# Second expert product in groups of eight blocks, two-bank sums, 32 lead tiles, and a moved broadcast of expert numbers

## The chip, the cores and the metric

The kernel runs on one core of one Trainium2 chip. The metric is the device time of one execution in microseconds; the time before is 3585.99 us, the median of three runs (3580.31, 3585.99 and 3586.01).

## The reference, cut to what matters

The model is one decoder block on 512 tokens of width 2048: a token mixer (convolution branch and state-space branch), then an expert mixer, then a final norm. The change touches the expert mixer alone. Each token picks 128 of 16384 single-neuron experts:

```python
best, pos = lax.top_k(cand, PEER_TOPK)            # 8 heads x 16 experts a token
expert = jnp.take_along_axis(cand_idx, pos, axis=-1)
gates = jax.nn.softmax(best, axis=-1)
act = jax.nn.gelu(jnp.einsum('td,thkd->thk', xb, u_tab[expert]))
out = jnp.einsum('thk,thkd->td', gates * act, v_tab[expert])
```

All is float32; the tables u and v have 16384 rows of 2048 numbers each (128 MB a table).

## The kernel before, in words

The token mixer and the routing (`route_half`, `top16`) take the first part of the span. The expert mixer then treats the 512 tokens in two ways at once.

**Dense tokens.** For the last 352 tokens (`ND`) every expert is computed, in 128 tiles of 128 experts (`NE`). `dense_u(j)` (line 858) multiplies tile j of table u with the tokens: 16 steps of 3 matmuls of 128x352 (lines 235 to 237), since each float32 product is made of a high and a low part (`split`, line 203: ACT casts the high part, DVE or POOL subtracts it to give the low part). ACT's Gelu gives `ga`. `weigh(j)` (line 1075) multiplies `ga` with the gates of the tile and splits the product into `wh` and `wl`. `dense_v(g, dc, ws)` (line 1117) multiplies four such tiles (`GRP` = 4) with a quarter `dc` of the width of table v: 48 matmuls of 128x352 into four one-bank sums (`ps_v`, 6 buffers), which DVE then adds to `acc` in SBUF one bank at a time (line 59, four additions of 128x352).

Until the gates exist, nothing can be weighed, so the first `LEAD` = 24 tiles run as `dense_u` alone and store `ga` in DRAM (`d_ga`). After `LAG` = 6 of them `transp_routes` turns the expert numbers and gates, and `gate_steps` then builds the dense gate matrix (4 tokens a step, 88 steps: one-hot products of 128x128 on PE, line 907) in the matmul stream of the next 16 tiles, and writes it to `d_g`. When the lead is over, groups 0 to 4 of `dense_v` run back to back (their tiles are re-read by `reload`), and from group 5 on one `dense_u` and one `dense_v` alternate.

**Gathered tokens.** For the first 160 tokens the 128 chosen rows are gathered: `gather_block` (line 967) is a generator whose steps are advanced by `pump_rows` between the dense units. A step issues one indirect DMA of 128 rows (1 MB, POOL's queue, line 963) two steps ahead and lets DVE multiply the oldest row tile (line 1011 for u, line 1022 for v). Three row buffers (`NROW`) serve the gathers, the token rows and the norm's scratch. `turn` makes token rows from columns with 16 PE transposes (line 985) each time a pass begins. The rows of one indirect DMA are held back behind `pace[0]`, the last elementwise POOL instruction recorded.

**Queues.** Each engine runs its own queue in order, but the framework that builds the queues may put a ready instruction ahead of one that is recorded earlier and still waits; the recorded order is a priority. SP issues the loads of both tables (line 222), the reloads (line 920) and the loads of token columns (line 973). POOL issues the gathers, the gate loads `gq` (line 1073) and `spread`, which copies 32 tokens' expert numbers over four partition groups through DRAM (lines 823 and 825). In the kernel before `spread(eidb, d_eb, eid1)` is recorded right after `expert_ids(eid1, 1)`, that is, before the first `dense_u`. The low parts of the first `UPOOL` = 10 tiles are made on POOL, as are every second low part of table v and the product with the gates (line 1081).

Of the kernel before, what the change touches and what calls it, by code (L numbers as in the profile page):

```python
# [15 lines left out]
T = 512  # L16
# [4 lines left out]
TB = 4  # L21
# [13 lines left out]
LEAD = 24  # L35
# [3 lines left out]
LAG = 6  # L39
GM = 1  # L40
TAIL = 2
NR = 18
NROW = 3
RLEAD = 1.5
RV = 1.0
UPOOL = 10
GRP = 4
# [106 lines left out]
def kernel(ctx, tc, xT, vecs, cst, w_in, conv_w_out, w_vg, w_out, w_q, keysT,  # L154
# [7 lines left out]
    vec = const.tile([128, V_END], F32, name="vec")  # L162
    cs = const.tile([128, C_END], F32, name="cs")
    ones = const.tile([128, 128], F32, name="ones")
# [11 lines left out]
    d_g = dram.tile([ND // 32, NE // GRP, 128, GRP, 32], F32, name="d_g")  # L176
    d_eb = dram.tile([GB, 128], I32, name="d_eb")
    d_gb = dram.tile([GB, 128], F32, name="d_gb")
    d_ga = [dram.tile([128, ND], F32, name=f"d_ga{j}") for j in range(LEAD)]

    yst = ExitStack()
# [44 lines left out]

    def proj_steps(ps, srcs, ah, al, eng=None, side=0.0):
        nk = 8 * len(srcs)
        for k in range(nk):
            if k % 8 == 0:  # L230
                hi, lo = load_w(srcs[k // 8], eng[k // 8] if isinstance(eng, tuple) else eng)
# [47 lines left out]
    rstd1 = const.tile([128, T], F32, name="rstd1", tag="rstd")  # L279
# [74 lines left out]
    rho4 = const.tile([128, 32], F32, name="rho4")  # L354
    ew = const.tile([128, 2, 224], F32, name="ew")
# [318 lines left out]
    rstd2 = const.tile([128, T], F32, name="rstd2", tag="rstd")  # L674
# [35 lines left out]

    scst = ExitStack()
    scp = scst.enter_context(tc.tile_pool(name="scp", bufs=8, reuse_waits="tile"))
    ij = const.tile([128, 2, TB, 8, 16], F32, name="ij")
    gt = const.tile([128, TB, 8, 16], F32, name="gt")
# [85 lines left out]
    zs = const.tile([128, TB * 8], F32, name="zs")  # L800

    def softmax():
# [5 lines left out]
        _mul(nc, g, g, zs[:, :, None].to_broadcast([128, TB * 8, 16]))  # L808

    eidx = con2.tile([128, HK], I32, name="eidx")  # L810
    eidb = con2.tile([128, GB], I32, name="eidb")
    gtb = con2.tile([128, GB], F32, name="gtb")
    sel = con2.tile([128, GB], F32, name="sel")
# [7 lines left out]
    def spread(o, d, src):  # L821

        nc.gpsimd.dma_start(d, src[:GB])
        for c in range(REP):
            nc.gpsimd.dma_start(o[c * GB:(c + 1) * GB, :], d[:, c * 32:(c + 1) * 32])

    eid1 = con2.tile([128, HK], I32, name="eid1")
    expert_ids(eidx, 0)
    expert_ids(eid1, 1)
    spread(eidb, d_eb, eid1)  # L830
# [8 lines left out]
    rp = ctx.enter_context(tc.tile_pool(name="rp", bufs=NR, side="right", reuse_waits="tile"))  # L839
    rowp = ctx.enter_context(tc.tile_pool(name="rowp", bufs=1, side="right", reuse_waits="tile"))  # L840
# [3 lines left out]
    def ps_v(shape=(512,)):  # L844
        return pp.tile([128, *shape], F32, name="pv", tag="v", bufs=6)
# [12 lines left out]
    def dense_u(j, eng=None, mid=None):  # L858
        pu = pp.tile([128, ND], F32, name="pu", tag="u", bufs=2)
        proj(pu, full(peer_ut, j), h2h, h2l, eng, mid=mid)  # L860
# [6 lines left out]
    tT = [ring(f"tT{i}") for i in range(3)]  # L867

    def transp_routes():
        softmax()  # L870
        spread(gtb, d_gb, gt[:, 1].rearrange("p h k -> p (h k)"))
# [29 lines left out]
    def gate_tokens(t0):  # L901
# [9 lines left out]
        if u0 == 28:  # L911
            for q in range(2):
                nc.sync.dma_start(d_g[t0 // 32, 16 * q:16 * q + 16].rearrange("q i j t -> i q (j t)"),
                                  stg[q].rearrange("p (q j) t -> p q (j t)", j=GRP))

    gars = {}

# [33 lines left out]
    def row_norm(o, x, g_dram):  # L951
# [4 lines left out]
        nc.vector.scalar_tensor_tensor(o, x, r, scr[:n], op0=ALU.mult, op1=ALU.mult)  # L956

    act = con2.tile([128, HK], F32, name="act")

# [7 lines left out]
    def gather_block(t0, n, ids, gates, steps):  # L967
        xt = [None]

        def load():  # L970
            xt[0] = row("xt").rearrange("p (k t) -> p k t", k=KD)
            if n == 128:
                nc.sync.dma_start(xt[0], d_x2[:, :, t0:t0 + 128].rearrange("k p t -> p k t"))
                return
            part = row("xp")[:, :KD * n].rearrange("p (k t) -> p k t", k=KD)
            nc.sync.dma_start(part, d_x2[:, :, t0:t0 + n].rearrange("k p t -> p k t"))
            for c in range(128 // n):
                nc.gpsimd.tensor_copy(xt[0][:, :, c * n:(c + 1) * n], part)

        def turn(scale):  # L980
            x2 = rowp.tile([128, D], F32, name="rows0", tag="rows", bufs=1)
            for q in range(4):
                pt = ps_v()
                for k in range(4):
                    nc.tensor.transpose(pt[:, k * 128:(k + 1) * 128], xt[0][:, 4 * q + k], ident)  # L985
                nc.scalar.activation(x2[:, q * 512:(q + 1) * 512], pt, AF.Copy, scale=scale)
            return x2

        load()
        for _ in range(3):  # L990
            yield
        x = turn(1.0)
        row_norm(x, x, gffn)
        todo = [(tab, e) for tab in (peer_u, peer_v) for e in range(steps)]
        live = []

        def ahead():
            if todo:
                tab, e = todo.pop(0)
                live.append(gather_row(tab, ids, e))  # L1000

        ahead()
        ahead()
        yield
        for i in range(steps):
            if i == steps - 2:
                load()
            else:
                ahead()
            g = live.pop(0)  # L1010
# [235 lines left out]
```

## Time and profile before

| | us |
|---|---|
| Time, median of three runs | 3585.99 |
| Profiled execution, own time | 3586.99 |
| Its span, first to last instruction | 3584.8 |
| First `dense_u` matmul | 1326.7 |
| Last `dense_v` matmul (then the last transposes and the norm) | 3567.9 |

The span is 2.2 us shorter than the profiled execution's own time, which is 1.0 us above the median. All positions below are microseconds from the span's first instruction.

### The profile page before, as it was taken

Reading aid. Unit: us, or ns where it says so; the run is one execution under the profiler, and the core shown is the slowest. Engines: PE = TensorE matmul, PEld = TensorE weight load, DVE = VectorE, ACT = ScalarE, POOL = GpSimd, SP = SyncE. Lnnn points to the kernel's source line nnn. Section 1 sums busy time; section 2 is a strip of 40 time slices with the busy share of each in tenths; the row PEclk is TensorE's granted clock in tenths of the full one; section 3 lists DMA queues with packets and bytes.
Section 4 is the critical chain, followed back from the end, with each engine's and each line's share of the span. In section 5 each row is a group of like instructions: output and inputs, shape, how many; then the busy total and the mean of one; then the engine's idle time right before and its main releaser. Section 6 shows DMA issues by size and latency. Waiting matters only on the chain. (4 is left out here: it accounts for less than half of the span.)

```text
span 3584.8 us, 50132 instructions
## 1 busy us (share of the span) xinstructions
PE 3416.8 (95%) x19091; PEld 3169.5 (88%) x19091; DVE 2856.6 (80%) x4147; ACT 1281.7 (36%) x2025; POOL 1452.8 (41%) x924
## 2 busy tenths in 40 slices
PE   8999999999999994997889999999999999999998
PEld 6888888888888884986789999999999999999998
DVE  7685848996535997796866999978999898797984
ACT  4234344325223331873223333333333333433333
POOL 1200000110003543343654666656666666465642
PEclk9999999999999997998899999999999999999999
DMA  5533444434444332699877989898989889897882
GB/s 176 154 108 114 129 123 123 140 125 129 135 147 132 113 111 69 188 302 320 273 252 264 357 333 355 340 337 317 356 347 343 335 342 358 285 361 295 344 303 95
DMA packets 261905, 845.30 MB, mean 236 GB/s; under 512 B 42640, under 2 KB 105184, under 8 KB 219904
## 3 DMA queue, kind: packets, MB, share of 16 engines
q1 hardware_dynamic: 189248, 433.25, 35.9%
q0 software_dynamic: 64352, 396.12, 29.4%
q10 hardware_dynamic: 8064, 12.72, 1.0%
q8 instruction: 150, 2.46, 0.3%
q14 instruction: 91, 0.75, 0.1%
HBM read 790.91 MB, written 51.09 MB: 235 GB/s over the span
## 5 line engine op out<-in xcount | busy, mean ns | idle before, releaser
L204 ACT CAST whi<-wraw 128x1024 fp32r<-128x1024 f32 x736 | 771.9, 1051 | 1792.1 <-PE pu L236 610.5
L205 DVE TENSOR_TENSOR wlo<-wraw,whi 128x1024 fp32r<-128x1024 f32 x556 | 743.1, 1351 | 207.6 <-ACT whi L204 206.5
L237 PE MATMUL pu<-h2h,wlo 128*128 128x352 f32 x2048 | 664.9, 325 | 67.7 <-POOL wlo L205 50.6
L1130 PE MATMUL pv<-wh,whi 128*128 128x352 f32 x2048 | 671.1, 328 | 47.8 <-DVE acc L59 29.9
L1132 PE MATMUL pv<-wh,wlo 128*128 128x352 f32 x2048 | 667.5, 326 | 4.7 <-DVE wlo L205 4.7
L235 PE MATMUL pu<-h2l,whi 128*128 128x352 f32 x2048 | 670.1, 327 | 1.1 <-ACT whi L204 1.1
L1131 PE MATMUL pv<-wl,whi 128*128 128x352 f32 x2048 | 667.5, 326 | 0.0
L236 PE MATMUL pu<-h2h,whi 128*128 128x352 f32 x2048 | 660.2, 322 | 0.0
L205 POOL TENSOR_TENSOR wlo<-wraw,whi 128x1024 fp32r<-128x1024 f32 x180 | 446.9, 2484 | 178.0 <-ACT whi L204 169.8
L1011 DVE SCALAR_TENSOR_TENSOR grow<-grow,rows 128x2048 f32<-128x2048 f32 x160 | 421.2, 2635 | 95.0 <-DMA grow<-in_peer_u_dram,eidx 83.3
L1022 DVE SCALAR_TENSOR_TENSOR rows<-grow,act,rows 128x2048 f32<-128x2048 f32 x160 | 427.8, 2674 | 85.1 <-DMA grow<-in_peer_v_dram,eidx 61.7
L237 PEld LDWEIGHTS pu<-h2h,wlo 128*128 128x128 f32 x2048 | 387.9, 189 | 71.9 <-POOL wlo L205 51.1
L1130 PEld LDWEIGHTS pv<-wh,whi 128*128 128x128 f32 x2048 | 390.9, 191 | 52.0 <-DVE acc L59 33.4
L1132 PEld LDWEIGHTS pv<-wh,wlo 128*128 128x128 f32 x2048 | 390.7, 191 | 5.1 <-DVE wlo L205 5.1
L1131 PEld LDWEIGHTS pv<-wl,whi 128*128 128x128 f32 x2048 | 392.4, 192 | 0.0
L235 PEld LDWEIGHTS pu<-h2l,whi 128*128 128x128 f32 x2048 | 386.8, 189 | 2.4 <-ACT whi L204 1.6
L236 PEld LDWEIGHTS pu<-h2h,whi 128*128 128x128 f32 x2048 | 387.7, 189 | 0.0
L235 PE MATMUL ps<-hl,whi 128*128 128x512 f32 x896 | 353.3, 394 | 9.2 <-ACT whi L204 9.2
L237 PE MATMUL ps<-hh,wlo 128*128 128x512 f32 x896 | 350.8, 392 | 0.4 <-DVE wlo L205 0.4
L236 PE MATMUL ps<-hh,whi 128*128 128x512 f32 x896 | 350.5, 391 | 0.0
L1081 POOL TENSOR_TENSOR ga<-gq,ga 128x352 f32<-128x352 f32 x104 | 171.1, 1646 | 434.8 <-ACT ga L862 418.4
L963 POOL DMA_INDIRECT grow<-in_peer_v_dram,eidx x128 | 247.0, 1930 | 76.5 <-DVE rows L1022 41.4
(338 smaller groups left out, 5084.7 us busy)
## 6 DMA issues: line engine op xcount, KB each, us to landing
wraw<-in_peer_ut_dram SPq DMA_DIRECT2D x256, 512.0 KB
wraw<-in_peer_vt_dram SPq DMA_DIRECT2D x256, 512.0 KB
wraw<-in_w_in_dram SPq DMA_DIRECT2D x112, 512.0 KB
d_g<-stg SPq DMA_DIRECT2D x22, 1024.0 KB
gq<-d_g POOLq DMA_DIRECT2D x32, 704.0 KB, 9.3
wraw<-in_w_vg_dram SPq DMA_DIRECT2D x32, 512.0 KB
wraw<-in_w_out_dram SPq DMA_DIRECT2D x32, 512.0 KB
wraw<-in_w_q_dram SPq DMA_DIRECT2D x32, 512.0 KB
```

Of the source, the lines that this page charges most:

```text
L204: ins = nc.scalar.copy(hi, src).ins
L205: low = (eng or nc.vector).tensor_tensor(lo, src, hi.bitcast(F32), op=ALU.subtract)
L235: nc.tensor.matmul(ps, hi[:, sl], al[k], start=k == 0, stop=False)
L236: nc.tensor.matmul(ps, hi[:, sl], ah[k], start=False, stop=False)
L237: nc.tensor.matmul(ps, lo[:, sl], ah[k], start=False, stop=k == nk - 1)
L963: nc.gpsimd.indirect_dma_start(out=g, out_offset=None, in_=tab, in_offset=bass.IndirectOffsetOnAxis(ap=ids[:, e:e + 1], axis=0))
L1011: nc.vector.scalar_tensor_tensor(g, g, 1.0, x, op0=ALU.mult, op1=ALU.mult, accum_out=act[:, i:i + 1])
L1022: nc.vector.scalar_tensor_tensor(x, g, act[:, i:i + 1], x, op0=ALU.mult, op1=ALU.add)
L1081: pace[0] = nc.gpsimd.tensor_tensor(g3, gq[0][:, :, j % GRP, :], g3, op=ALU.mult).ins
L1130: nc.tensor.matmul(pvs[i], hi[:, s], wh, start=e == 0, stop=False)
L1131: nc.tensor.matmul(pvs[i], hi[:, s], wl, start=False, stop=False)
L1132: nc.tensor.matmul(pvs[i], lo[:, s], wh, start=False, stop=e == GRP - 1)
```

## The change

1. **Groups of eight.** `GRP` goes from 4 to 8. `dense_v` makes 96 matmuls a call over eight tiles; the last two tiles close the four sums one after the other. In the steady part two `dense_u` come between two `dense_v`.
2. **Two banks a sum.** `ps_v((2, 512))` holds two sums in two banks, with 3 such buffers instead of 6 of one bank; DVE adds 2x352 columns in one instruction. `acc` is no longer loaded; the first group adds to `res`, a row buffer loaded with the residual.
3. **32 lead tiles.** `LEAD` 24 to 32, `LAG` 6 to 11, `TAIL` 2 to 5, `UPOOL` 10 to 11. The gate steps again take 16 tiles (11 to 26). The first eight tiles are weighed within the last four lead tiles.
4. **Rows turned once.** The columns of the 160 gathered tokens are loaded at tile 0, transposed at tiles 4 and 6 and stored as rows (`d_xr`); each pass then loads its rows and ACT scales them. No transposes remain in the passes.
5. **Expert numbers sent later.** `spread(eidb, ...)` goes into `transp_routes`, recorded behind tile 11 (j = 10), together with `spread(gtb)` and a new `spread(rtb)`, all behind `pace[0]`.
6. **Engines and queues.** The product with the gates moves from POOL to DVE, and all low parts of table v go to DVE. The gate load is recorded just before the first `weigh` that needs it (before: behind the last `weigh` of the preceding group). Both tables are read through one `Stream` that records loads and splits ahead (4 and 2, after the lead 6 and 3). `d_g` is laid out so that a write is 8 KB in one piece a partition (before: pieces of 512 B). The gathers are paced by a new one-column POOL copy (`mark`) behind each `ga` and behind the last sum of each `dense_v`.
7. **Steps of the gather.** 327 steps instead of 336: 0.8 a tile in the last five lead tiles, 17.6 in the first three groups, 13.5 in the last group, and the rest evenly.

The diff, cut to its core:

```diff
-LEAD = 24
+LEAD = 32
-LAG = 6
+LAG = 11
-TAIL = 2
-NR = 18
+TAIL = 5
+NR = 4
-RLEAD = 1.5
-RV = 1.0
-UPOOL = 10
-GRP = 4
+RLEAD = 0.8
+RV = 0.8
+REND = 4.5
+UPOOL = 11
+QG = 4
+GRP = 8
...
-    spread(eidb, d_eb, eid1)
...
-        return pp.tile([128, *shape], F32, name="pv", tag="v", bufs=6)
+        return pp.tile([128, *shape], F32, name="pv", tag="v", bufs=3)
...
     def transp_routes():
         softmax()
-        spread(gtb, d_gb, gt[:, 1].rearrange("p h k -> p (h k)"))
+        with after(pace[0]):
+            spread(eidb, d_eb, eid1)
+            spread(rtb, d_rb, rt[:, 1:2], 1)
+            spread(gtb, d_gb, gt[:, 1].rearrange("p h k -> p (h k)"))
...
+    def weigh(j, ga):
+
+        if j % QG == 0:
+            load_gates(j // QG)
+        if j < LEAD:
+            ga = gars.pop(j) if j in gars else reload(j)
+        g3 = ga.rearrange("p (b t) -> p b t", t=32)
+        nc.vector.tensor_tensor(g3, gq[0][:, :, j % QG, :], g3, op=ALU.mult)
+        p = wgp[j // GRP % 2]
+        wh, wl = (p.tile([128, ND], F32R, name=n, tag="w") for n in ("wh", "wl"))
+        split(wh, wl, ga)
+        return wh, wl
...
+    def paced(ap):
+
+        mark = con2.tile([128, 1], F32, name="mark", tag="mark", bufs=2)
+        pace[0] = nc.gpsimd.tensor_copy(mark, ap[:, 0:1]).ins
...
-        pvs = [ps_v((ND,)) for _ in range(4)]
-        for e, i in [(e, i) for e in range(2) for i in range(4)] + [(e, i) for i in range(4) for e in (2, 3)]:
+        pairs = [ps_v((2, 512)) for _ in range(2)]
+        pvs = [pairs[i // 2][:, i % 2, :ND] for i in range(4)]
+        last = range(GRP - 2, GRP)
+        order = [(e, i) for e in range(GRP - 2) for i in range(4)] + [(e, i) for i in range(4) for e in last]
...
-        for i in range(4):
-            a = acc[:, 4 * dc + i]
-            _add(nc, a, pvs[i], a)
-        if g == NE // GRP - 1:
+        for h in range(2):
+            a, pv = acc[:, 4 * dc + 2 * h:4 * dc + 2 * h + 2], pairs[h][:, :, :ND]
+            _add(nc, a, pv, a if g else res[dc][:, 2 * h:2 * h + 2])
+        paced(acc[:, 4 * dc + 3])
...
-    rate = (steps_g - gi[0] - RV * LEAD) / (NE - LEAD - 4)
+    rate = (steps_g - gi[1] - RV * (LEAD - GRP - 2) - 3 * REND) / (NE - LEAD) 
```

## Rows read from the trace of the kernel before

**Rows 1.** The page: span, busy time and share of each engine, instructions.

```profile
span 3584.8 us, 50132 instructions
PE 3416.8 (95%) x19091; PEld 3169.5 (88%) x19091; DVE 2856.6 (80%) x4147; ACT 1281.7 (36%) x2025; POOL 1452.8 (41%) x924
```

**Rows 2.** Windows: stretch, length, busy us (instructions) of each engine, PE clock, DMA share, GB/s.

```profile
1326.70:1357.50 30.80, 30.80 (x197) 30.80 (x195) 30.49 (x131) 11.18 (x17) 13.35 (x6) 1.00 0.48 147
1357.50:1406.70 49.20, 0.33 (x3) 0.04 (x2) 45.36 (x242) 1.32 (x2) 2.96 (x3) 0.55 0.01 4
1441.10:1651.00 209.90, 197.93 (x1410) 195.00 (x1409) 184.96 (x222) 157.61 (x444) 88.19 (x50) 0.98 0.84 267
1651.00:1675.30 24.30, 17.31 (x97) 16.45 (x95) 16.33 (x15) 4.83 (x6) 5.68 (x4) 0.86 0.96 344
1675.30:1897.10 221.80, 171.76 (x963) 167.69 (x963) 149.66 (x165) 54.37 (x68) 120.76 (x72) 0.90 0.75 257
1897.10:2376.60 479.50, 479.50 (x2988) 479.36 (x2987) 426.58 (x420) 156.42 (x187) 294.49 (x158) 1.00 0.89 339
```

**Rows 3.** Windows as above: 100 us of steady work, and two stretches where passes change.

```profile
2100.00:2200.00 100.00, 100.00 (x625) 100.00 (x625) 92.24 (x92) 32.58 (x39) 61.76 (x33) 1.00 0.89 343
2376.60:2400.40 23.80, 18.08 (x103) 17.79 (x102) 18.30 (x18) 6.50 (x11) 12.46 (x8) 0.86 1.02 362
3272.30:3297.70 25.40, 20.20 (x115) 19.91 (x114) 11.04 (x14) 7.27 (x12) 12.41 (x10) 0.87 0.72 243
```

**Rows 4.** PE's waits over the span: who waited for whom, us, times, longest.

```profile
PE pu L237 <- POOL wlo L205: 50.6, 2, 48.9
PE pv L985 <- DMA xt<-d_x: 5.7, 1, 5.7
PE pv L985 <- POOL xt L978: 5.2, 1, 5.2
```

**Rows 5.** Timelines of POOL and DVE around 1403: start, us, instruction [idle before, releaser].

```profile
1347.11 2.45 POOL L205 TENSOR_TENSOR wlo<-wraw,whi 128x1024 fp32r<-128x1024 f32 x1 [1.41 <-ACT whi L204]
1403.73 0.53 POOL L823 DMA_DIRECT2D d_eb<-eid  x1 [54.18 <-DVE eid L819]
1403.21 0.23 DVE L819 CAST eid<-ef 128x128 int32<-128x128 f32 x1
```

**Rows 6.** Groups by line, PE, 1424 to 1651: count, busy us, mean ns, idle before.

```profile
L907 PE MATMUL pv<-oj,oi 128*128 128x128 f32 x704 | 95.1, 279 | 1.5 <-POOL oi L894 1.0 <-ACT oi L897 0.6
```

**Rows 7.** PE's waits from 1675.3 to 1897.1, groups 0 to 4 of the second product.

```profile
PE pv L1130 <- DVE acc L59: 27.5, 11, 5.2
PE pv L1130 <- ACT wh L204: 10.6, 1, 10.6
PE pv L1130 <- ACT whi L204: 7.3, 1, 7.3
PE pv L1132 <- DVE wlo L205: 4.7, 1, 4.7
```

**Rows 8.** DVE's timeline in that stretch: row steps, sums, low parts.

```profile
1810.97 2.29 DVE L1011 SCALAR_TENSOR_TENSOR grow<-grow,rows 128x2048 f32<-128x2048 f32 x1 [3.16 <-DMA grow<-in_peer_u_dram,eidx]
1813.19 1.81 DVE L59 TENSOR_TENSOR acc<-pv,acc 128x352 f32<-128x352 f32 x4
1814.92 1.21 DVE L205 TENSOR_TENSOR wlo<-wraw,whi 128x1024 fp32r<-128x1024 f32 x1
1816.06 0.52 DVE L205 TENSOR_TENSOR wl<-gar,wh 128x352 fp32r<-128x352 f32 x1
```

**Rows 9.** Groups by line, DVE, steady part 1897.1 to 3475: busy us, mean ns, idle before.

```profile
L1022 DVE SCALAR_TENSOR_TENSOR rows<-grow,act,rows 128x2048 f32<-128x2048 f32 x160 | 427.8, 2674 | 85.1 <-DMA grow<-in_peer_v_dram,eidx 61.7 <-DMA grow<-in_peer_v_dram,eidb 21.5 <-ACT rows L986 1.7
L1011 DVE SCALAR_TENSOR_TENSOR grow<-grow,rows 128x2048 f32<-128x2048 f32 x121 | 326.5, 2699 | 56.3 <-DMA grow<-in_peer_u_dram,eidx 44.6 <-DMA grow<-in_peer_u_dram,eidb 11.6
L59 DVE TENSOR_TENSOR acc<-pv,acc 128x352 f32<-128x352 f32 x401 | 189.4, 510 | 5.0 <-PE pv L1132 4.2 <-issue 0.9
```

**Rows 10.** DMA issues: queue, count, KB each, median us from issue to landing.

```profile
gq<-d_g POOLq DMA_DIRECT2D x32, 704.0 KB, 9.3
```

More of the change, by code (lines that the diff above doesn't have):

```diff
@@ L965, in gather_row, with gather, ahead, load @@
         return g
[L967 to L976, printed above, removed]
-            for c in range(128 // n):
-                nc.gpsimd.tensor_copy(xt[0][:, :, c * n:(c + 1) * n], part)
+    def gather():
+        blocks = [(0, GA, eidx, gta, HK, rt[:, 0:1]),
+                  (GA, GB, eidb, gtb, HK // REP, rtb)]
+        passes = [(b, tab) for b in blocks for tab in (peer_u, peer_v)]
+        todo = [(tab, b[2], e) for b, tab in passes for e in range(b[4])]
+        live, xt, gain = [], [], []
+        def ahead():
+            if todo:
+                live.append(gather_row(*todo.pop(0)))
+        def load(b):
+            t0, n = b[:2]
+            x = row("xt")
+            for c in range(128 // n):
+                nc.sync.dma_start(x[c * n:(c + 1) * n], d_xr[t0:t0 + n])
+            xt.append(x)
+        def load_gain():
+            gain.append(row("gain"))
+            nc.gpsimd.dma_start(gain[0], gffn[None, :].to_broadcast([128, D]))
@@ L980, in turn @@
         def turn(scale):
             x2 = rowp.tile([128, D], F32, name="rows0", tag="rows", bufs=1)
[L982 to L986, printed above, removed]
-            return x2
-        load()
+            nc.scalar.activation(x2, xt.pop(), AF.Copy, scale=scale)
@@ L990, in gather_block @@
+            return x2
+        load(blocks[0])
+        load_gain()
         for _ in range(3):
             yield
[L992 to L1003, printed above, removed]
-        yield
[L1005 to L1010, printed above, removed]
-            nc.vector.scalar_tensor_tensor(g, g, 1.0, x, op0=ALU.mult, op1=ALU.mult, accum_out=act[:, i:i + 1])
-            yield
@@ L1013, in gather_block @@
-        with after(last_ga[0]):
-            nc.scalar.activation(act[:, :steps], act[:, :steps], AF.Gelu_apprx_tanh)
-        _mul(nc, act[:, :steps], act[:, :steps], gates)
-        x = turn(1.0 if n == 128 else float(n) / 128)
-        ahead()
-        yield
-        for i in range(steps):
-            ahead()
-            g = live.pop(0)
-            nc.vector.scalar_tensor_tensor(x, g, act[:, i:i + 1], x, op0=ALU.mult, op1=ALU.add)
-            yield
-        if n < 128:
-            for _ in range(3):
-                yield
-            y = row("ysum")
-            for q in range(4):
-                pt = ps_v()
-                nc.tensor.matmul(pt[:n], sel, x[:, q * 512:(q + 1) * 512], start=True, stop=True)
-                nc.scalar.copy(y[:n, q * 512:(q + 1) * 512], pt[:n])
-            x = y
@@ L1063 @@
     acc = accp.tile([128, KD, ND], F32, name="acc")
[L1064 to L1065 removed]
+    wgp.append(ctx.enter_context(tc.tile_pool(name="wgb", bufs=2 * GRP, side="right", reuse_waits="tile")))
+    for kind, n in (("raw", 2), ("hi", 1), ("lo", 1)):
+        rings[kind].append((vp, n))
         turn_of[kind] = 0
[L1068 to L1086 removed]
+    tabs.loads, tabs.splits = 6, 3
     tail = {}
```

256 lines of the change are left out of this document (180 added, 76 removed).

## The prediction, on record before the changed kernel ran

> **What bounds the kernel now.** I read the page's engine shares first, then windows, then who waits for whom. TensorE (PE) is busy 95% of the 3584.8 us span [rows 1], so a change can gain only where PE stands or runs slowly, and the question is how much of the expert part is that. A steady 100 us window holds about 624 matmuls without a gap [rows 3], 0.1603 us each, so one unit of 48 matmuls is 7.69 us. The expert part has 128 + 128 such units (the change leaves that product as it is: 96 matmuls in a call, half as many calls): 256 x 7.69 = 1969 us. From the first of them at 1326.7 to the last at 3567.9 pass 2241 us, so 272 us are something else. I find them by stretch [rows 2, 3]:
> - *The hole*, 1357.5 to 1406.7: 49.2 us for 3 matmuls. PE waits 48.9 us for a low part that POOL should make [rows 4]; POOL stands 54.18 us before the first DMA of the broadcast, until DVE's last routing step at 1403.21 has made the expert numbers [rows 5]. A DMA issue, and not arithmetic, holds up the tables' low parts.
> - *The gate stage*, 1441.1 to 1651.0: 704 narrow gate matmuls are true work, 8 for each of 88 steps [rows 6]. PE idles 12.0 us of 209.9 there [rows 2].
> - *The lead's end*, 1651.0 to 1675.3: 97 matmuls are 15.5 us, so 8.8 us are lost [rows 2].
> - *Groups 0 to 4*, 1675.3 to 1897.1: 960 matmuls are 153.9 us, so 67.9 us are lost [rows 2]; 50.1 us of it are waits [rows 7], and the rest is the clock, granted at 0.90 over the stretch [rows 2], which is 1.2 GHz for a part of it and 2.4 GHz for the rest. 22.6 us of waits belong to the start (weighed tiles and first low parts), 27.5 us in 11 waits to sums that DVE has not yet added [rows 7]. In proportion to the idle time that makes 30.6 us for the start and 37.3 us for the sums.
> - *Two passes' beginnings* [rows 3]: 103 matmuls (16.5 us) take 23.8, and 115 (18.4 us) take 25.4; 7.3 + 7.0 us. PE waits for token columns that it must turn [rows 4].
> - The rest of the steady part has no gaps: PE is busy 479.50 of 479.50 us [rows 2], with DVE at 426.6 us (0.89) and DMA at 0.89.
>
> **Part by part, on the profiled span of 3584.8 us.**
>
> *Broadcast moved, LAG 11.* The DMA that holds POOL goes behind tile 11's low parts in POOL's queue. What is queued behind it then are POOL's shares of the first gate steps, not the tables. Tiles 4 to 10 need nothing of the routing, so PE works through the hole: 11 x 7.69 = 84.6 us, until 1411.3, and routing ends at 1403.2 at present. Gain 49.2 - 0.5 (3 matmuls) = 48.7 us. The cover is the 11 tiles; with only 6 it would be gone. Now POOL's low parts run beside the routing's DVE work, for some 12 of them. Price from the trace: with 6 POOL instructions DVE made 131 instructions in 30.8 us; with POOL standing, 242 in 45.4 us busy [rows 2]. At the second rate 131 take 24.6 us, so 6 POOL instructions cost DVE about 6 us, 1.0 us each, and 12 move the routing's end by 12 us, to 1415, a few us behind tile 10's end. Softmax, transposes and one-hots follow as now. The three broadcasts are 15 issues at about 0.53 us [rows 5], 8 us of POOL's queue; the first two of them need only the expert numbers and can run while tile 10 does. Behind the third stands POOL's share of the first gate steps, and behind that PE. I charge 5 us for all of it (bounds 0 and 16).
>
> On that point a rule speaks against the change: the Trainium skill, SBUF — State Buffer, section "Who interferes with whom", says that a DVE instruction with two SBUF inputs and a GpSimd instruction that reads SBUF exclude each other for a whole instruction. If that struck at each of the 12 low parts of 2.45 us [rows 5], routing would end 29 us later and the charge would be some 21 us instead of 5. The rows show less, 1.0 us for each; I go by them.
>
> *Gate stage.* Again 16 tiles and 88 steps, so its matmuls stay. The row steps leave this stretch (1.5 a tile before, none until tile 27), and DVE, at 185 of 209.9 us [rows 2], gets room. The larger pieces of d_g relieve the DMA (0.84). Of 12.0 us idle I take 8 off (bounds 0 and 12). One transposition of each block instead of two saves 32 transposes, about 4 us at the 0.135 us that a narrow matmul takes here (95.1 us busy by 704 [rows 6]).
>
> *Lead's end and start of the groups.* The last gate step is recorded in tile 26; five tiles, 38 us, then cover the landing of d_g and gq (9.3 us [rows 10]) and the weighing of the first eight tiles. The extra work there is small: on DVE eight gate products at about 0.52, eight low parts `wl` at 0.52 and tables at 1.21 each [rows 8]. Of 8.8 + 30.6 = 39.4 us I leave 6: gain 33 (bounds 19 and 39). The res load replaces the load of acc; it takes one of three row buffers, and the lower pace of the first group leaves room for that.
>
> *Sums in groups 0 to 2.* 20 calls become 12, with 11 boundaries instead of 19; each costs 37.3 / 19 = 2.0 us now. A sum of two banks costs between 0.51 (one 352-column sum [rows 9]) and 1.02; from 0.52 at 352 columns and 1.21 at 1024 [rows 8] a column is 1.03 ns, and I take 0.51 + 352 x 1.03 ns = 0.87 us. The first buffer comes free later than before: 12 instead of 18 matmuls ahead of the end (0.96 us) and 0.36 us for the longer sum, 1.3 us in all. At the worst each boundary waits that longer, which with the clock's share (67.9 / 50.1 = 1.36) is 2.0 + 1.8 = 3.8 us, 42 us in all. But what keeps DVE from the sums is a row step ahead of them that waits for its gather (3.16 us [rows 8]); there are fewer row steps now (0.8 instead of 1.0 in 7.7 us), and a row is asked for two steps, so more than one call of 15.4 us, before its use, against landings of the kind of gq's 9.3 us [rows 10]. I take 12 us: gain 25 (bounds -5 and 37).
>
> *Passes.* Rows come by DMA and ACT scales them; PE waits no more: gain 14.
>
> *Steady part.* Here nothing is to be gained, so the question is what becomes late next. DVE for two units (15.4 us): before 0.89 x 15.4 = 13.7 us. After: rows (327 - 4 - 17.6 - 13.5) / 96 = 3.04 a pair (before 2.91) at 2.3 us, since the long ones lie beside POOL's elementwise work, which goes (mean 2.67 [rows 9], alone 2.29 [rows 8]): 7.0; four low parts 4.8; gate product and wl 1.04; sums 0.87 instead of four at 0.51: 13.7 us. What POOL gives DVE to do is what the sums and the free port give back. Waits for gathers, (61.7 + 21.5 + 44.6 + 11.6) us over 102 pairs [rows 9], add 1.4: 15.1 of 15.4. DMA carries 3.04 + 2 MB of tables + 0.17 MB of gates: 5.46 million bytes in 15.4 us, 355 GB/s, against 339 at share 0.89 [rows 2], so share 0.93. Both just fit. The marks are one-column copies on a POOL that has lost its elementwise work; the gathers behind them wait for the end of a unit, as they do now. I charge 5 us (bounds -5 and 65; the upper end is 96 pairs at the 0.68 us by which 5.46 million bytes at 340 GB/s exceed 15.4).
>
> *Last group.* 13.5 steps in three calls, of which about 10 are rows; an estimate from a landing of 9 to 10 us like gq's, the row step and its issue is 13 us a turn of a buffer, so three buffers give a row every 4 or 5 us, so DVE stands in front of the sums more often. PE waits 6 us (bounds 0 and 20). The final norm is as before.
>
> Sum: -48.7 + 5 - 8 - 4 - 33 - 25 - 14 + 5 + 6 = -116.7; span 3468. The profiled execution ran 2.2 us above its span and the median lies 1.0 us below it, so I forecast **3469 us**.
>
> **Rivals.**
> *A. The steady part slips* (chance 0.16). DVE's 15.1 of 15.4 us is tight, DMA too. Each 0.5 us too much per pair costs 48 us; at 0.7 to 1.0 us it is 65 to 96, giving 3530 to 3560 (the 5 us charged above are in it). For it: 0.93 DMA share, three row buffers that must now turn over in 15.2 instead of 15.9 us. Against it: before, DVE at 0.89 plus waits left PE without a gap; 2376.6 to 2400.4 moved 362 GB/s [rows 3].
> *B. The hole stays in part* (0.06). If another issue takes POOL's front, or the routing ends as late as 1432, 20 to 49 us come back: 3490 to 3518.
> *C. Slower: DVE waits for the gate load* (0.06). The load of gq is recorded right in front of the DVE product that needs it, and behind the mark that waits for ga. If the queue keeps that order, DVE stands 9.3 us [rows 10] once in four tiles; in four pairs DVE has 4 x 0.3 us to spare, so about 8 us of each reach PE, and 24 such loads cost 194 us: 3663. From 4.9 us a load that reach PE (117 / 24) the change loses. Before, the load was recorded ahead by a group's end and POOL stood for it. Against it: queues do not keep the recorded order; POOL ran tables' low parts, the last at 1347, ahead of the broadcast, which was recorded before them [rows 5], and the buffer of gq is free three units (23 us) before the product.
> *D. The broadcast and the sums do nothing else than shift waits* (0.02): about 3580.
>
> **How the numbers follow.** Forecast 0.70, with its own range 3430 to 3505. The range that should hold 8 in 10 takes in A's lower half and B: 3430 to 3545. About 0.2% (7 us) can be told from no change by this measurement. Faster 0.92 (forecast, A, B), same 0.02 (D), slower 0.06 (C).
>
> **What would show it.** Right: PE's wait for POOL's low part of 48.9 us is gone and PE is dense from 1326.7 to about 1411; PE's waits for DVE sums between the lead and the steady part fall from 27.5 us to some 9; no waits at transposes in the steady part; DVE row steps at 2.3 us. Wrong: steady units above 7.75 us (A), DVE waiting on gq (C), POOL standing on a DMA before 1411 (B). The forecast falls if the steady part needs more than about 7.9 us a unit.

## The result, and the profile after

The changed kernel takes 3828.48 us (median of 4 runs, 3820.59 to 3838.85) beside 3586.00 us (median of 4, 3580.31 to 3592.45) for the kernel before: a ratio of 1.068 with a 95% interval of 1.0665 to 1.0698. It is 6.8% slower; the forecast was 3469 us, 3.3% faster, and the measured time lies 284 us above the upper end of the range. The profiled execution has a span of 3821.1 us. Its page, as in [rows 1] (span, busy time and share of each engine):

```profile
span 3821.1 us, 49889 instructions
PE 3514.3 (92%) x19059; PEld 3257.5 (85%) x19059; DVE 2712.8 (71%) x4006; ACT 1256.4 (33%) x2009; POOL 1004.8 (26%) x832
```

DVE and POOL have less to do than before (2712.8 against 2856.6 us, 1004.8 against 1452.8 [rows 1]), and still PE waits more. The windows by stretch answer [rows 2, 3]; the columns are the stretch, its length, the busy us (and instructions) of PE, PEld, DVE, ACT and POOL, then PE's granted clock, the DMA share and GB/s:

```profile
1325.30:1407.70 82.40, 82.29 (x516) 81.43 (x514) 81.61 (x331) 31.86 (x41) 44.91 (x19) 1.00 0.57 185
1407.70:1619.60 211.90, 206.10 (x1483) 205.00 (x1482) 167.18 (x218) 163.20 (x469) 50.08 (x45) 0.99 0.59 198
1619.60:1661.10 41.50, 39.74 (x242) 39.16 (x242) 16.30 (x21) 13.53 (x20) 8.55 (x8) 1.00 0.79 261
1661.10:1886.90 225.80, 200.67 (x1154) 196.73 (x1153) 145.36 (x165) 63.95 (x78) 39.73 (x38) 0.94 0.77 266
1886.90:3712.00 1825.10, 1601.48 (x9217) 1579.75 (x9216) 1256.10 (x1107) 474.69 (x587) 628.63 (x461) 0.93 0.80 290
```

The first four stretches are the hole, the gate stage, the lead's end and groups 0 to 2; the fifth is the steady part, groups 3 to 14, up to the last group. Up to 1886.9 the changed kernel has done 56 units of 48 matmuls (32 first, 24 second product); the kernel before had done 44 at 1897.1. That is 12 units of 7.69 us and 10.2 us, 102.5 us ahead. Everything is lost behind it. In the steady part (the last row) 9217 matmuls at the dense 0.1603 us [rows 3] are 1477.5 us and take 1825.1: 347.6 us lost. PE stands for 223.6 us of that; the other 124 us are longer matmuls, at a granted clock of 0.93 over the stretch, that is, at 1.2 GHz for a part of it. DVE's share (1256.1 of 1825.1, 0.69) and DMA's (0.80) fell from 0.89 each [rows 2]. No engine is as full as it was, so the loss points at a wait.

Who waits for whom over the span (us, times, longest):

```profile
PE pv L1233 <- DVE wlo L210: 178.2, 53, 6.2
PE pu L270 <- DVE wlo L210: 50.8, 24, 5.4
PE pv L1231 <- DVE acc L61: 32.8, 11, 9.6
DVE rows L1116 <- DMA grow<-in_peer_v_dram,eidx: 282.1, 47, 9.9
DVE grow L1113 <- DMA grow<-in_peer_u_dram,eidx: 227.4, 58, 9.6
POOL mark L1142 <- DVE acc L61: 757.2, 64, 20.2
POOL mark L1142 <- ACT ga L916: 492.4, 54, 13.1
```

Read it from PE upward. PE waits 229 us for low parts that DVE makes. DVE waits 608.6 us for gathered rows (the two lines and 49.7 + 49.4 us for the second token block's rows). In the steady part alone it is 553.4 us, where the kernel before waited 139.4 [rows 9]. The gathers are issued by POOL, and POOL stands 757 us at a one-column copy whose input is a sum that DVE has to make. So the waits form a ring. One turn of it, POOL's timeline first (start, us, instruction, [idle before, releaser]):

```profile
2088.97 0.91 POOL L1142 COPY mark<-ga 128x1 f32<-128x1 f32 x1 [10.59 <-ACT ga L916]
2090.04 1.79 POOL L1058 DMA_INDIRECT grow<-in_peer_u_dram,eidx  x1 [0.16 <-DVE grow L1113]
...
2108.08 1.03 POOL L1142 COPY mark<-acc 128x1 f32<-128x1 f32 x1 [11.35 <-DVE acc L61]
2109.27 1.80 POOL L1058 DMA_INDIRECT grow<-in_peer_u_dram,eidx  x1 [0.16 <-issue]
```

and DVE's of the same stretch, with PE's last matmul of that call of the second product:

```profile
2097.34 2.29 DVE L1113 SCALAR_TENSOR_TENSOR grow<-grow,rows 128x2048 f32<-128x2048 f32 x1 [0.97 <-DMA grow<-in_peer_u_dram,eidx]
...
2104.84 2.28 DVE L1113 SCALAR_TENSOR_TENSOR grow<-grow,rows 128x2048 f32<-128x2048 f32 x1
...
2107.05 0.89 DVE L61 TENSOR_TENSOR acc<-pv,acc 128x704 f32<-128x704 f32 x1
...
2119.83 2.29 DVE L1113 SCALAR_TENSOR_TENSOR grow<-grow,rows 128x2048 f32<-128x2048 f32 x1 [9.62 <-DMA grow<-in_peer_u_dram,eidx]
```

```profile
2100.72 0.32 PE L1233 MATMUL pv<-wh,wlo 128*128 128x352 f32 x1
```

The row step at 2097.34 ends at 2099.6 and leaves its row buffer free. The next gather could start then; it starts at 2109.27, because POOL's queue holds the copy of `acc` ahead of it, and `acc` is added by DVE at 2107.05, behind two more row steps. DVE stands 9.62 us for it, until 2119.83, with the low parts and sums of the next product queued behind. That makes the sums late, the sums make the mark late, and the mark makes the gathers late. PE pays for it in waits for low parts, but it is hardly a link of the ring: PE had ended this call by 2101.04, 6.9 us before the sum was done, and in the whole steady part DVE waited for PE before a sum only once:

```profile
DVE acc L61 <- PE pv L1233: 1.0, 1, 1.0
```

By the start times in the trace, the mark behind a sum starts on average 10.4 us after PE's last matmul of its call (5.3 to 16.9 us, the 48 calls of the steady part).

### The profile page after: what moved, and what is told of

The parts are those of the page before. It is cut to its first block, busy times and chain, and to the rows that moved or that the text cites. A ratio compares the mean times of both kernels' runs of the same rounds, so it can differ in the third digit from the quotient of the medians.

```text
span 3821.1 us, 49889 instructions
## 1 busy us (share of the span) xinstructions
PE 3514.3 (92%) x19059; PEld 3257.5 (85%) x19059; DVE 2712.8 (71%) x4006; ACT 1256.4 (33%) x2009; POOL 1004.8 (26%) x832
## 5 line engine op out<-in xcount | busy, mean ns | idle before, releaser
L210 DVE TENSOR_TENSOR wlo<-wraw,whi 128x1024 fp32r<-128x1024 f32 x682 | 830.6, 1225 | 227.1 <-ACT whi L209 226.7
L1233 PE MATMUL pv<-wh,wlo 128*128 128x352 f32 x2048 | 707.2, 345 | 178.3 <-DVE wlo L210 178.2
L1231 PE MATMUL pv<-wh,whi 128*128 128x352 f32 x2048 | 704.4, 344 | 34.8 <-DVE acc L61 32.8
L1232 PE MATMUL pv<-wl,whi 128*128 128x352 f32 x2048 | 696.5, 340 | 0.0
L1116 DVE SCALAR_TENSOR_TENSOR rows<-grow,act,rows 128x2048 f32<-128x2048 f32 x160 | 375.7, 2348 | 332.2 <-DMA grow<-in_peer_v_dram,eidx 282.1
L1113 DVE SCALAR_TENSOR_TENSOR grow<-grow,rows 128x2048 f32<-128x2048 f32 x160 | 366.2, 2289 | 277.3 <-DMA grow<-in_peer_u_dram,eidx 227.4
L1231 PEld LDWEIGHTS pv<-wh,whi 128*128 128x128 f32 x2048 | 418.3, 204 | 39.2 <-DVE acc L61 36.0
L209 ACT CAST wh<-ga 128x352 fp32r<-128x352 f32 x96 | 46.7, 486 | 834.7 <-DVE ga L987 834.7
L1142 POOL COPY mark<-acc 128x1 f32<-128x1 f32 x64 | 84.5, 1320 | 757.2 <-DVE acc L61 757.2
L1142 POOL COPY mark<-ga 128x1 f32<-128x1 f32 x101 | 97.5, 966 | 506.5 <-ACT ga L916 492.4
```

The lines of the kernel that those rows point to most:

```text
L209: ins = nc.scalar.copy(hi, src).ins
L210: low = (eng or nc.vector).tensor_tensor(lo, src, hi.bitcast(F32), op=ALU.subtract)
L1113: nc.vector.scalar_tensor_tensor(g, g, 1.0, x, op0=ALU.mult, op1=ALU.mult, accum_out=act[:, i:i + 1])
L1116: nc.vector.scalar_tensor_tensor(x, g, act[:, i:i + 1], x, op0=ALU.mult, op1=ALU.add)
L1142: pace[0] = nc.gpsimd.tensor_copy(mark, ap[:, 0:1]).ins
L1231: nc.tensor.matmul(pvs[i], hi[:, s], wh, start=e == 0, stop=False)
```

## Experiments

Besides the mark, two other causes were held possible: the longer call of the second product, and the low parts that DVE took over from POOL. All of these compute the whole result, and each differs from its parent by the lines shown. A time without a range is that of one run. For scale, the four runs of experiment 8 lie between 3471.3 and 3497.3 us, so a difference of some 20 us between single runs shows little.

**1. The mark behind the sums, away.** From the changed kernel:

```
         for h in range(2):
 ...
-        paced(acc[:, 4 * dc + 3])
```

> The changed kernel without the one-column POOL copy behind the last sum of each dense_v; the copies behind each ga stay. Nothing of the result is left out. Theory 1 (late release): three row gathers of each period of four table tiles (two u, a double v) wait for that copy although their row buffers are free; DVE then stands in a row step in front of the low parts that PE needs, about 6 us in each of 48 periods. So the span falls from 3821 to some 3500 to 3560, DVE's waits for gathers (609 us) fall below 250, and a double v takes about 16 us instead of 22. Theory 2 (groups of eight themselves bunch DVE's work): the span stays within 60 of 3821. Theory 3 (all low parts on DVE behind row steps, POOL idle): within 100 of 3821, PE's waits for DVE's low parts stay above 150 us.

Measured: 3531.1 us, 297 us less, with the kernel before at 3583.1 beside it. DVE's waits for gathers and PE's for low parts:

```profile
DVE rows L1116 <- DMA grow<-in_peer_v_dram,eidx: 88.1, 50, 5.6
DVE grow L1113 <- DMA grow<-in_peer_u_dram,eidx: 87.6, 58, 5.8
PE pu L270 <- DVE wlo L210: 34.6, 29, 3.6
```

All waits of DVE for gathers are 213.9 us now, below the 250 expected. The 100 us window of [rows 3]:

```profile
2100.00:2200.00 100.00, 97.73 (x602) 96.87 (x601) 80.68 (x79) 29.94 (x37) 36.70 (x25) 1.00 0.89 330
```

One copy in each double call, 1.0 us long in the median (0.2 to 3.3), carries more than the whole loss of 242 us: without it the rest of the change is 52 us faster than the kernel before.

**2. No marks at all.** Also without the two `paced(ga)`, the gathers free of any mark:

> The changed kernel with no pacing of the gathers at all: neither the copies behind ga and the sums, nor the order behind pace. A gather starts when its row buffer is free. Theory 1: as e1 or somewhat better, 3480 to 3560. If instead gathers need pacing because bursts of 1 MB delay the table loads, PE waits for ACT's casts or DVE's low parts behind late loads, and the span is above e1's by 20 us or more. Theories 2 and 3: within 100 of 3821.

Measured: 3628.9 us, 98 us above experiment 1 and above the expected range too. Two things show. First, with nothing to hold it back, a gather of the first rows stands in POOL's queue ahead of low parts of table u, and POOL stands until DVE has made the expert numbers. This is the old hole in part, by another issue (rival B's mechanism):

```profile
1404.56 1.00 POOL L1058 DMA_INDIRECT grow<-in_peer_u_dram,eidx  x1 [28.43 <-DVE eidx L857]
PE pu L270 <- POOL wlo L210: 25.8, 3, 23.5
```

Second, in the steady part the row steps run ahead as fast as buffers come free and are missing later. The window of [rows 3], and one behind it:

```profile
2100.00:2200.00 100.00, 93.71 (x563) 91.64 (x561) 87.12 (x86) 28.55 (x36) 37.07 (x26) 0.98 0.99 383
2300.00:2500.00 200.00, 200.00 (x1247) 200.00 (x1246) 92.25 (x97) 68.15 (x80) 7.00 (x6) 1.00 0.54 173
```

First DMA is at 0.99 and DVE at 0.87, and PE has gaps; then PE is dense, with DVE at 0.46 and DMA at 0.54. That the tables come late is not what the run shows: from 1900 to 2300 DVE waits 1.4 us for high parts, and the median landing of the tables' loads from 1900 to 3400 is 7.8 and 7.2 us, against 7.7 and 7.2 in experiment 1. PE waits there for low parts (29.3 us), which share DVE's queue with the row steps. So some pacing is worth having; what it waits for is the question.

**3. Every second low part of the second product on POOL.** From the changed kernel, marks kept; the pieces with odd `p2` are split with `nc.gpsimd` and do not move the pace:

```
-                    yield peer_vt[g * GRP // 4 + p2 // 2, dc, p2 % 2], None
+                    yield peer_vt[g * GRP // 4 + p2 // 2, dc, p2 % 2], nc.gpsimd if p2 % 2 else None
```

> The changed kernel with every second low part of table v on POOL, as in the kernel before; these instructions don't pace the gathers, the marks stay. Theory 3: PE's waits for DVE's low parts (229 us) fall by half or more, span 3650 to 3720. Theory 1: the marks still release the gathers late, DVE's waits for gathers stay above 500 us, and the other low parts still stand behind them: span within 60 of 3821, or above it since POOL's elementwise work lengthens DVE's.

Measured: 3878.2 us, slower still. POOL's waits at the mark, and the page's busy times:

```profile
POOL mark L1143 <- DVE acc L61: 619.0, 56, 15.7
PE 3519.0 (91%) x19059; PEld 3241.4 (84%) x19059; DVE 2713.8 (70%) x3878; ACT 1253.8 (32%) x2009; POOL 1256.6 (32%) x960
```

DVE's waits for gathers stay at 598 us (245.7 + 238.1 + 66.2 + 47.9), and PE's for DVE's low parts fall only from 229 to 187 us. DVE makes 128 instructions less, but its busy time does not fall (2713.8 against 2712.8 us), since the others get longer beside POOL's elementwise work. So giving the low parts back to POOL does not relieve DVE. That their move to DVE is not the cause follows from this run together with experiment 1, which leaves all low parts on DVE and regains the whole loss.

**4. Groups of 4 in the changed kernel**, marks kept (`GRP = 4`, with the loops over `jn` and the rate scaled to it):

> The changed kernel with groups of four: one u and one v (48 matmuls) in turn, sums still two banks at a time, marks as in the changed kernel (behind ga and behind the last sum), twice as many sums. Theory 2: the loss of the steady part goes, span 3450 to 3530. Theory 1: the mark behind the sums now comes every 15.4 us and releases 1.5 rows, not every 31 us with 3, so part of the loss goes, span 3520 to 3700. Theory 3: within 100 of 3821.

Measured: 3765.0 us, 63 us less. That misses the ranges of theories 1 and 2; it lies in theory 3's, against which experiments 1 and 3 speak. POOL waits 1029.4 us for sums, DVE 417.7 for gathers. The length of the call is a part of the price, not its root: beside experiment 8 (3481.4 us), which is this kernel without the mark, the mark costs 284 us in groups of 4 as well.

**5. The same mark, waiting for something else.** Experiments 1 and 2 take a mark away, and so also change POOL's order. This one keeps order and number of marks and gathers and changes only what the third mark reads: a table's high part, made by ACT; the mark is recorded in the middle of the double call.

```
             if e // 2 == len(pcs):
                 pcs.append(tabs.take())
+                if e == 4:
+                    paced(tabs.ready[-1][0].bitcast(F32))
 ...
-        paced(acc[:, 4 * dc + 3])
```

> The changed kernel with the third mark of each period kept at its place in POOL's queue, but reading a table's high part (made by ACT, which waits only for PE to free a buffer in the middle of the double unit) instead of DVE's last sum. POOL's order of marks and gathers is the same as in the changed kernel. Theory 1 (the loss comes from a mark that waits for DVE, so that a late DVE makes its own gathers later): 3490 to 3560 us, DVE's waits for gathers near 200 us as in the run without that mark. Rival (three marks in a period, whatever they wait for, release the gathers too late): above 3700 us, waits for gathers near 600 us.

Measured: 3537.2 us (median of 4, 3533.1 to 3538.2), a ratio of 0.987 (0.9854 to 0.9887) to the kernel before. POOL's waits at the marks, and DVE's for rows:

```profile
POOL mark L1142 <- ACT ga L916: 539.3, 93, 13.5
POOL mark L1142 <- ACT whi L209: 119.7, 22, 14.4
DVE grow L1113 <- DMA grow<-in_peer_u_dram,eidx: 111.2, 55, 10.8
DVE rows L1116 <- DMA grow<-in_peer_v_dram,eidx: 83.8, 50, 5.5
```

291 us come back by pointing the mark at ACT instead of DVE. POOL stands no less at `ga` than in the changed kernel (492.4 us); it is the wait for DVE that counts. The new mark is also released earlier: by the start times in the trace it starts on average 2.1 us before PE's last matmul of its call, where the mark behind the sums starts 10.4 us after it. It is still near the end of PE's call, and what went is the time by which DVE's sums trail PE. A mark at the very end of the call that waits for PE alone was not run.

**6. The mark put into the kernel before.** Nothing else is changed there; POOL still has its low parts and gate products, and the calls are groups of 4:

```
         for i in range(4):
             a = acc[:, 4 * dc + i]
             _add(nc, a, pvs[i], a)
+        mark = con2.tile([128, 1], F32, name="mark", tag="mark", bufs=2)
+        pace[0] = nc.gpsimd.tensor_copy(mark, acc[:, 4 * dc + 3, 0:1]).ins
```

> The kernel before, with one thing added: a one-column copy on POOL behind the last sum of each call of the second product, and the gathers recorded after it wait for it, as in the changed kernel. Theory 1 (a mark that waits for DVE's sums is enough by itself): slower by 80 to 300 us, 3665 to 3885 us, DVE's waits for gathers far above 139 us. Rival (it hurts only where POOL has lost its elementwise work, or only with groups of eight): 3570 to 3620 us.

Measured: 3990.5 us, 406 us slower, more than the 80 to 300 expected. The same ring shows:

```profile
POOL mark L1137 <- DVE acc L59: 961.8, 116, 12.0
DVE rows L1022 <- DMA grow<-in_peer_v_dram,eidx: 345.1, 46, 9.5
DVE grow L1011 <- DMA grow<-in_peer_u_dram,eidx: 253.2, 48, 8.8
```

The mark is enough by itself, without any other part of the change. Here POOL's own low parts are queued behind it too (PE waits 60.9 us for them), so not all of the 406 us is the ring.

**7. The hole part alone**, in the kernel before (28 lead tiles, gate work from tile 10 on, the broadcast of the expert numbers recorded behind `pace[0]`):

```
-LEAD = 24
+LEAD = 28
-LAG = 6
+LAG = 10
-    spread(eidb, d_eb, eid1)
 ...
+        with after(pace[0]):
+            spread(eidb, d_eb, eid1)
```

> The kernel before with the broadcast of the expert numbers recorded behind tile 9's low parts and gate work from tile 10 on (28 lead tiles), nothing else. Prediction's step: 48.7 us gained less 5 charged. Theory (that part was right, and its gain is kept to the end): 3530 to 3550 us, PE's wait of 48.9 us for POOL's low part gone. Rival (what is gained there is given back later, by DMA or DVE): 3560 to 3590 us.

Measured: 3553.3 us, 31 us less than before, 3 us above the expected range. PE's waits from 1320 to 1450:

```profile
PE pv L878 <- DVE ij L798: 14.6, 2, 11.3
```

and the window of the old hole:

```profile
1326.70:1403.00 76.30, 76.21 (x480) 75.92 (x478) 75.68 (x290) 25.91 (x34) 42.36 (x18) 1.00 0.51 155
```

The wait of 48.9 us [rows 4] is gone and PE is dense, but with a cover of 10 tiles instead of 11 PE then waits 14.6 us for the routing's last step.

**8. Groups of 4 without the mark behind the sums.** Experiment 1 with the edits of experiment 4, run once and then four times more:

> Groups of 4 and no mark behind the sums: is the group of eight itself worth anything? With the mark, groups of 4 gained 58 us. If the group of eight does what was claimed (half the sums and half the boundaries; 4 sums of 0.88 us more in a period of 30.8 us), this comes out slower than the 3531 us of the run without the mark: 3570 to 3680 us, with PE's waits for DVE's sums up. If the size of the group is worth nothing: 3515 to 3545 us.

> The same kernel as in the look at groups of 4 without the mark behind the sums (3482 us there), timed in rounds: 3475 to 3490 us, 2.6 to 3.0% under the kernel before.

Measured: 3482.1 us in the first run, then 3481.4 us (median of 4, 3471.3 to 3497.3) beside 3585.5 for the kernel before: ratio 0.9715 (0.9679 to 0.975). The expectation fell: groups of eight cost 50 us, they do not gain. This version is faster than both kernels of the case. A long stretch of it (the last group without `dense_u` and most of the steady part) and that of the change of token blocks, as windows of the profiled one of the four runs:

```profile
1873.20:3359.00 1485.80, 1461.09 (x9025) 1455.97 (x9024) 1315.46 (x1177) 462.38 (x569) 630.70 (x400) 1.00 0.92 347
3093.60:3141.00 47.40, 35.34 (x194) 33.89 (x193) 35.61 (x35) 14.41 (x18) 16.00 (x14) 0.93 0.88 330
```

Lost against 0.1603 us a matmul: 39.1 us in the long stretch (34.6 in the first run), 72.2 in experiment 1's steady part (9218 matmuls in 1549.8 us). That is 33 of the 50 us; the rest lies in the early groups (5), the lead's end (3) and the last group (7). A possible reason shows in POOL's timelines. Experiment 1:

```profile
2554.70 0.97 POOL L1058 DMA_INDIRECT grow<-in_peer_v_dram,eidx  x1 [0.23 <-DVE rows L1116]
2566.50 2.13 POOL L1142 COPY mark<-ga 128x1 f32<-128x1 f32 x1 [10.83 <-ACT ga L916]
```

and experiment 8, first run:

```profile
2542.56 2.12 POOL L1058 DMA_INDIRECT grow<-in_peer_v_dram,eidx  x1 [1.71 <-DVE rows L1116]
2550.19 0.18 POOL L1142 COPY mark<-ga 128x1 f32<-128x1 f32 x1 [5.51 <-ACT ga L916]
```

In groups of eight two `ga` come in one period and then none for a double call, so POOL stands 10.8 us with buffers free and then issues three gathers in a row; with groups of 4 the pause is 5.5 us.

**9. Is it the bunching?** Experiment 8 with the mark behind only every second `ga`:

```
-                        paced(ga)
+                        if jn % 2:
+                            paced(ga)
```

> Groups of 4 without the mark behind the sums, with the mark behind ga only at every second table, so one release in 30.8 us instead of two. Why do groups of eight cost some 49 us? Theory B (they bunch the gathers: POOL stands about 11 us at a mark with the row buffers free, then three gathers start at once and DVE gets rows and low parts at once): this comes near the groups of eight, 3515 to 3570 us, with DVE's waits for gathers from about 60 us up to 150 or more. Rival (it is the double call itself, its order on DVE or its sums, whatever the marks): 3475 to 3500 us.

Measured: 3501.9 us, between the two expectations. In the same long stretch 9027 matmuls take 1501.2 us, 54.2 lost, 15 more than in experiment 8. So the coarser release explains at most some 15 of the 33 us; it is one run, 4.6 us above the slowest of experiment 8, and DVE's waits for gathers rise only to 115 us where theory B had 150 or more. The rest stays open: a third mark in the double call (experiment 5) did not bring it back, so it is not the spacing alone.

**10. Fewer row steps in the last group** (experiment 8 with `REND = 2.0` instead of 4.5):

> Groups of 4 without the mark behind the sums, with 2.0 row steps instead of 4.5 in each call of the last group; the 7.5 steps go to the 96 pairs before it (0.08 a pair, 0.18 us of DVE). The last four calls took 46 us where dense ones take 31. If DVE's rows in the last group are the cause: 8 to 15 us less at the end, against up to 10 us more before: 3465 to 3485 us. If the steady part has no room: above 3490 us.

Measured: 3498.6 us, 17 us slower. The last four calls are dense now (35.4 us instead of 43.5 in experiment 8), 8 us less as expected. The part ahead of them, where 0.08 rows a pair were added, takes 1502.8 us instead of 1485.8. That suggests a steady part without room, and does not show it: one of the four runs of experiment 8 took 3497.3 us.

**11. No row steps in the groups that run off stored `ga`** (experiment 8 with `RV = 0.0` instead of 0.8):

> Groups of 4 without the mark behind the sums, and no row steps in the groups that run off stored ga (RV 0): their rows go to the steady part. Only the stretch of those groups is read, 24 units that took 214 us (185 when dense), with 19 us of PE waits for sums. Prediction's claim (row steps ahead of the sums keep DVE from them): waits for sums under 6 us, stretch 185 to 198 us. Rival (the first low parts and reloads keep DVE busy): waits for sums stay above 12 us. The whole: 3475 to 3530 us.

Measured: 3509.1 us in all. The window of those groups (214.2 us in experiment 8):

```profile
1657.10:1856.00 198.90, 189.91 (x1155) 189.32 (x1154) 131.22 (x158) 63.74 (x79) 8.89 (x9) 0.97 0.67 214
```

and PE's waits for sums in it (19.2 us, 7 times, in experiment 8):

```profile
PE pv L1231 <- DVE acc L61: 9.0, 2, 6.4
```

The first expectation was missed narrowly, and the rival's too: with the row steps gone half of the waits for sums go, and 15 of the 29 us that the stretch had lost. The other half stays open.

Four row buffers instead of three were not tried; whether a fourth would hide a late mark is open.

## Why the prediction was wrong, step by step

*Steady part: the step that failed.* "The marks are one-column copies on a POOL that has lost its elementwise work; the gathers behind them wait for the end of a unit, as they do now." The mark was priced by its own length and by the count of instructions on POOL. What counts is what it waits for, and whose work that is. Before, the gathers stood behind POOL's gate products and low parts, and these wait for ACT. From the kernel before, 1897.1 to 3475:

```profile
POOL ga L1081 <- ACT ga L862: 393.0, 95, 9.5
```

No entry of DVE's sums stands there. The changed kernel put one in, and with it DVE became the one that releases its own inputs. The prediction's own rule for an added wait (what is queued behind it, and who waits for that) was not worked through for this one: behind it stand the gathers, behind those DVE's row steps, and behind those, in DVE's own queue, the low parts that PE needs and the sums that the mark needs. The charge was 5 us with an upper bound of 65, and that bound was DMA's: the mark had no term of its own. Measured are 348 us lost in the steady part. Of these, 72 remain without the mark (experiment 1). Experiments 1, 5 and 6 show the cause from three sides: without the mark -297 us, the mark pointed elsewhere -291, the mark alone in the kernel before +406.

The claim that a row is asked for early enough ("more than one call of 15.4 us, before its use") fell with it. In the turn shown above a free buffer waited 9.7 us for the mark, and the gather was issued 10.6 us before the row step that needed it. The sums of work were right: row steps at 2.29 and 2.35 us, a sum of 704 columns at 0.89, low parts at 1.22. DVE's 1256.1 us over 96 pairs are 13.1 us a pair, where 13.7 were worked out. The waits were not: 1.4 us a pair for gathers in the working, 5.8 measured (553.4 over 96).

*Rival A* named the right place, "the steady part slips", and sized it at 65 to 96 us by work per pair. Without the mark it is right in kind: 72 us lost in experiment 1. *Rival C*, the only one on the slower side, had the right form (POOL's queue holds a load behind a mark, DVE stands for it) at the wrong load: DVE waited 8.3 us for `gq` in the whole span. The same reasoning applied to the gathers, six in a period of two first and one double second units, would have pointed at the loss.

*Broadcast moved, LAG 11.* Right. PE is busy 82.29 of 82.40 us where 48.9 us were a wait [rows 2, 4]. The charge of 5 us was the right size: PE waits 5.7 us in three waits once tile 11 is done. The expert numbers come at 1408.25 instead of 1403.21 [rows 5], 5.0 us later, where the working had 12. That smaller number is luck. At 1326.7 the changed kernel's routing was some 8 us ahead, an estimate from 19 rounds of the search for the largest eight left on DVE instead of 24, and 1.6 us a round. The price itself was about as worked out: beside POOL's 18 low parts, four kinds of DVE instruction took 12.3 us more in all than in the kernel before. Single instructions are held, as one of these kinds shows, before and after (shortest, median and longest, ns):

```profile
L793 DVE TENSOR_TENSOR oh<-pf,cs x12: 676/684/685, 1346.6 to 1400.8; 128x512 f32<-128x512 f32 x12
L828 DVE TENSOR_TENSOR oh<-pf,cs x12: 680/686/2889, 1337.4 to 1405.8; 128x512 f32<-128x512 f32 x12
```

The rule of the Trainium skill, SBUF — State Buffer, section "SBUF: two separate sides", by which two such instructions exclude each other for their whole length, would have made it 29. The trace agrees that it happens, 2.89 us instead of 0.69 beside a low part of 2.63, but not that it strikes at every low part: eight DVE instructions of this stretch are held so.

*Gate stage.* Right: PE idles 5.8 us of 211.9, where it idled 12.0 of 209.9 [rows 2]: 6 us less, where 8 were taken off.

*Lead's end and start of the groups.* Right: 242 matmuls in 41.5 us lose 2.7 where 8.8 were lost, and the waits at the start are 3.0 us instead of 22.6 [rows 7].

*Sums in groups 0 to 2.* Wrong by about 24 us. PE waits there for sums, nine times:

```profile
PE pv L1231 <- DVE acc L61: 22.0, 9, 4.2
```

against 27.5 in eleven [rows 7]. 1154 matmuls are 185.0 us and take 225.8. In proportion to the waits (3.0 and 22.0 us) 5 of the 41 lost belong to the start, so some 36 stay where 12 were allowed. The working said that fewer row steps would leave DVE free for the sums. Fewer boundaries came, but each wait is as long as before (2.4 us). In groups of 4 the row steps are about half of it (experiment 11).

*Passes.* Right at the two places named, and a third was overlooked. In experiment 8 the changes from table u to table v lose 3.5 and 0.6 us (2425 to 2500 and 3255 to 3300), where the kernel before lost 7.3 and 7.0 [rows 3]. At the change of token blocks between them the kernel before lost 3.8 us (247 matmuls in 43.4), and experiment 8 loses 16 (194 matmuls in 47.4, shown there):

```profile
3067.00:3110.40 43.40, 40.55 (x247) 39.96 (x246) 29.97 (x41) 21.03 (x27) 15.33 (x13) 0.96 0.86 288
3255.00:3300.00 45.00, 44.97 (x277) 44.17 (x276) 38.16 (x33) 15.45 (x19) 21.37 (x12) 1.00 0.96 343
```

There DVE stands 5.4 us (first run of experiment 8) for a gain that is being loaded, and 5.8 us before the new block's first row step. So about 10 of the 14 us came, and 12 us went where no term was set.

*Last group.* 6 us were charged. The last eight units take 92.4 us (3712.0 to 3804.4). Four units are 30.8 us, and the last four with the output's transposes 35.4 where they are dense (experiment 10), so 26 us are lost, and 16 of the 81.9 in experiment 1. Row steps before the sums are the likely reason: in groups of 4 the end is dense with 2.0 steps a call (experiment 10); for groups of eight it was not run.

The sum: to 1886.9 the forecast had 113.7 us of gain and 102.5 came. From there it had 3 us of gain, and 339 us were lost against the kernel before (236 at the end, and the 102.5 ahead). The 353 us between 3468 and 3821 are what fell short in these two (11 and 342), and 297 of it is one line.

## What to carry to other kernels

A wait added to a queue is priced by the engine that releases it and by what stands behind it, followed until the chain ends or comes back to where it began. Pace a prefetch by an engine that does not use what is fetched: here marks on ACT's output gained 98 us over no marks, and one on the consumer's output closed a ring and lost 297. Larger groups save instructions, but they also space the events by which other work is released: without the ring, groups of eight were 50 us slower than groups of 4, and the spacing explains at most a part of that.

## What the runs showed of the hardware

A gather of one row in each of 128 partitions took nearly the same time from issue to landing under different loads of the DMA engines. The DMA issues from 1900 to 3400 (queue, count, median us from issue to landing), changed kernel first, then no marks at all:

```profile
grow<-in_peer_v_dram,eidx POOLq DMA_INDIRECT x128, 9.9
```

```profile
grow<-in_peer_v_dram,eidx POOLq DMA_INDIRECT x128, 9.4
```

Over that stretch the DMA engines moved 286 GB/s in the first and 318 in the second. In the kernel before, experiment 1 and experiment 8 (336, 342 and 352 GB/s) it is 9.8, 9.2 and 9.7 us. So the lighter DMA load of the changed kernel did not make up for a late issue.

Moving 128 low parts of table v from DVE to POOL saved DVE no busy time (2713.8 against 2712.8 us, experiment 3): its row steps took 2.48 and 2.56 us on average instead of 2.29 and 2.35.

One core alone moved 383 GB/s over 100 us at a DMA share of 0.99 (experiment 2). The Trainium skill, Perfetto Trace Analysis, section "Engine Utilization", gives 358 GB/s for a core's share of memory bandwidth and says that a single active core can exceed it up to its DMA engines' 435; the row agrees that the share is exceeded, and at 0.99 busy it stays well under the upper figure.
